# One layer of a hybrid trunk: squares and rotated inputs moved ahead, table copies spread and paired

## The chip, the cores and the metric

The kernel runs on one core of one Trainium2 chip. The metric is device time in microseconds (us) of one launch, which computes the whole layer. A core has five engines with a queue of instructions each: TensorE (PE; its weight loads are shown as PEld), VectorE (DVE), ScalarE (ACT), GpSimd (POOL) and SyncE (SP), which mostly issues DMA transfers. An engine takes its queue in order; engines wait for each other through semaphores. Matrix products land in PSUM, eight banks of 512 float32 per partition, and are evicted by DVE or ACT to SBUF, 128 partitions of on-chip memory.

## The reference

x is 2048 tokens (32 rows of a grid, 64 columns) by 1024, in float32; c is one vector.

```python
mod = silu(c) @ w_ada + b_ada
shift, scale, gate = split(mod, 3)
h = rmsnorm(x, norm_w) * (1 + scale) + shift
proj = h @ w_in + b_in      # na q,k,v,z (512 each); ml q,k,v,o,z (512 each); 16 gates
na = neighbourhood_attention(q, k, v, rpb) * silu(na_z)   # 8 heads of 64, window 8 x 16 on the grid
qk = silu(short_conv(concat(ml_q, ml_k)))                 # 5 taps along the tokens
hm = mlstm(forward) + flip(mlstm(flipped))                # 4 heads of 128, with sigmoid(ml_o)
ml = layernorm(hm) * ml_norm_w * silu(ml_z)
y = concat(na, ml) @ w_out
out = rmsnorm(x + gate * y) * final_norm_w
```

The attention adds a bias rpb[head, dy, dx] to the scores and masks what lies outside the window.

## The kernel before

Every large product is made in float32 precision of three products of half the width: a factor is split into a high part (hhi, whi) and the rest (hlo, wlo), and hi·hi, lo·hi and hi·lo are added up in PSUM. A k-step below is a slice of 128 of the inner 1024. The tokens are four groups (g = 0 to 3) of 512, or 16 tiles of 128.

**Token stage (`start`, 0 to about 145 us).** Group 0's rows are loaded, normalised and transposed on PE; the shift and scale columns are dot products on DVE (L264) and one-column products on PE (`mod`, L366); five `dense` products run ahead of them (L347). Its h is multiplied at once with two blocks of weights in PSUM (L418). Groups 1 to 3 go another way: a transposed copy of x (xt, `load_t`) is loaded, and h is made from it by `make_h` (L390): DVE multiplies with scale and with rb (L394), ACT adds the shift and rounds to hhi (L395), DVE takes the rest, hlo (L396). rb holds 1/rms of each token in every partition. It comes from four `square`s on ACT over plain rows of x (L260, one sum per token), `roots` (eleven small DVE operations, L270 and L1380 to L1395), four diagonal matrices on DVE (L285), and four products of ones with them on PE (L290). The diagonals and rb together are `spread`; rb is issued by its `run`.

A weight block is 256 columns; `vo_group(h, slot, g)` makes four tiles of 128 tokens by 256, 24 products each (L599 to L601, `tok_tile`), adds the bias on DVE (L671) and sends the stage tile stvo to DRAM (d_ck). After each eviction it takes a step of `self.chain`, which is how the next group's h (`next_h`) or weights (`next_w`) get between. `vo_first(g)` makes block 0's four tiles at once, k-step by k-step (L654), so that h may arrive block by block; `vo_group(0, 0, g, firsts)` then only evicts them. For group 0, `vo_group(2, 2, 0)` uses a third block, w_extra, split in two halves (L212 on ACT, L213).

**Token blocks (`tok_blocks`, to about 320 us).** Blocks 2 to 5 for all groups; the mLSTM's gates and decays run alongside as a chain (`decays`: dec loads from d_mneg on SP, mask on POOL, exponent on ACT). The attention's bias tables are made by DMA alone: d_e[head, column, dy, key column] gets rows of the bias at shifted places (`tables_columns`, 48 copies, L704), and d_t[head, query, key] gets rows of d_e (`tables_rows`, 72 copies, L726).

**Convolution blocks (`conv_blocks`, to about 480 us).** 32 tiles of 128 channels by 512 tokens (`pc`, 24 products); ACT moves each to u, DVE applies the taps (acc_k, acc_q, L982 to L984), ACT the silu (L986); k's are transposed on PE (kt, L995), moved by ACT (stk, L997) and stored by SP (L989, L999). `gated_out` loads rows of w_out (wraw, L910), multiplies them by gate on DVE and stores them (L918).

**mLSTM and the rest of the projections (to about 950 us)**, with products pq (L1042) between the small products of the chunks; `turn` transposes normalised chunks (ht, L1338) and `end` multiplies them into zt (L1344). **Attention and output (to the end):** units of two heads and 128 queries; scores pS (L1533), DVE adds the table and takes the minimum (L1541, pbuf; signs are turned), ACT exponentiates (L1542), PE transposes (pT) and multiplies with v (pO), then the output product y (L1621).

The order is partly a scheduler's (priorities follow the order in which the code calls), partly fixed: `manual_schedule` in the token stage keeps the order of the code, and `behind(step, other)` (L1161) puts a step behind another in order alone, without a semaphore.

## Time and profile before

| | us |
|---|---|
| three runs: median (lowest, highest) | 1324.9 (1324.34, 1331.62) |
| profiled execution | 1328.02 |
| its span, first to last instruction | 1326.2 |
| PE busy in it | 1282.2 |
| mean granted TensorE clock | 0.993 |

The three runs lie apart by more than the profiled one does from their median, so it is compared with itself first. In a row of the timeline the columns are the start, the duration, engine, line, operation, output and inputs, shape and count; in brackets the idle time of the engine just before and what ended it. A group's row gives the count with the shortest, median and longest duration in ns, and the first and last start. A row of windows gives, for a stretch, its length, each engine's busy time with its count, the granted clock of TensorE (1.00 is full), the DMA engines' busy share and GB/s. SPq and ACTq are queues that issue DMAs. x4 in a row joins four instructions that follow each other.

### The profile page before, as it was taken

The page shows a single profiled execution, that of the slowest core. Times are in us where ns is not written, and L with a number is a line of the kernel's source. Part 1 is how long each engine was busy: PE and PEld are TensorE (multiplying, and loading weights), DVE is VectorE, ACT ScalarE, POOL GpSimd, SP SyncE. Part 2 cuts the span into 40 slices and gives each one's busy share as a digit, 9 for nine tenths or more (in the row PEclk, how much of TensorE's full clock was granted, in tenths as well). Part 3 has the DMA queues.
Part 4 walks back from the last instruction along what each step waited for, and adds up shares of the span by engine and source line. Part 5 has one row for each costly group of instructions (what it writes and reads, how often), then busy time and mean ns, then how long its engine had stood idle before and what let it go on. Part 6 is the DMA issues. An engine that isn't in the chain of part 4 may idle for free.

```text
span 1326.2 us, 23060 instructions
## 1 busy us (share of the span) xinstructions
PE 1282.2 (97%) x8158; PEld 1099.5 (83%) x8158; DVE 791.9 (60%) x2445; ACT 536.6 (40%) x1175; POOL 194.9 (15%) x255
## 2 busy tenths in 40 slices
PE   8999999999999999999999999999998999999996
PEld 7998999998888787888888888888776777778785
DVE  6766352112556577166778778777547566766663
ACT  4543423553213322123323323333346555565561
POOL 0000102342000000111212002121202211212211
PEclk9999999999999999999999999999999999999998
DMA  9799966899276685445756767746779877868871
GB/s 365 256 293 319 239 199 144 219 246 231 77 174 183 167 215 158 147 132 165 211 151 212 229 181 215 234 140 194 196 236 240 214 184 195 201 175 194 191 185 48
DMA packets 236964, 263.86 MB, mean 199 GB/s; under 512 B 31142, under 2 KB 192294, under 8 KB 236850
## 3 DMA queue, kind: packets, MB, share of 16 engines
q1 hardware_dynamic: 152430, 189.92, 51.1%
q0 software_dynamic: 20496, 36.21, 11.1%
q10 hardware_dynamic: 63924, 36.27, 9.5%
q8 instruction: 64, 1.05, 0.3%
q14 instruction: 50, 0.41, 0.1%
HBM read 177.80 MB, written 92.72 MB: 204 GB/s over the span
## 4 chain that ended last, share of the span: by engine, by line
PE 62%; DMA 21%; issue 7%; DVE 5%; ACT 2%; POOL 1%; SPq 1%; ACTq 0%; POOLq 0%; DVEq 0%
PE pq L1042 19%; PE y L1621 10%; DMA tab<-d_t 5%; PE pc L600 4%; PE pc L599 4%; PE pc L601 4%; DMA d_ck<-dec 3%; PE pT L1561 2%; PE pO L1576 2%; DMA dec<-d_mneg 2%; PE pi L1283 2%; PE px L1281 2%; PE pS L1533 2%; PE pvo L599 2%; PE pvo L600 2%
## 5 line engine op out<-in xcount | busy, mean ns | idle before, releaser
L1042 PE MATMUL pq<-hhi,whi_a 128*128 128x512 f32 x512 | 208.7, 408 | 0.8 <-ACT u L947 0.8
L1042 PE MATMUL pq<-hlo,whi_a 128*128 128x512 f32 x512 | 209.0, 408 | 0.0
L1042 PE MATMUL pq<-hhi,wlo_a 128*128 128x512 f32 x512 | 207.4, 405 | 0.0
L1042 PEld LDWEIGHTS pq<-hhi,whi_a 128*128 128x128 f32 x512 | 97.3, 190 | 17.8 <-ACT u L947 1.3
L1042 PEld LDWEIGHTS pq<-hhi,wlo_a 128*128 128x128 f32 x512 | 97.1, 190 | 16.3
L1042 PEld LDWEIGHTS pq<-hlo,whi_a 128*128 128x128 f32 x512 | 97.1, 190 | 16.1 <-issue 0.5
L1563 ACT ACTIVATE pt<-pT 96x384 f32<-96x384 f32 (+3 forms) x128 | 65.8, 514 | 87.0 <-PE pT L1561 80.8
L1542 ACT ACTIVATE pbuf<-pbuf,mn 128x480 f32<-128x480 f32 (+5 forms) x128 | 76.0, 595 | 52.4 <-DVE mn L1541 52.2
L1621 PE MATMUL y<-hhi,whi_a 128*128 128x512 f32 x256 | 90.7, 416 | 0.5 <-ACT whi_a L1591 0.5
L1621 PE MATMUL y<-hhi,wlo_a 128*128 128x512 f32 (+1 forms) x272 | 90.6, 399 | 0.2 <-ACT y L1628 0.2
L1016 POOL TENSOR_TENSOR wlo_a<-rawq,whi_a 128x1024 fp32r<-128x1024 f32 x19 | 45.6, 2398 | 292.3 <-ACT whi_a L1015 265.1
L1541 DVE CUSTOM_DVE_ANT_0 pbuf<-pS,tab 128x480 f32<-128x480 f32 (+5 forms) x128 | 62.8, 540 | 37.3 <-PE pS L1533 30.9
L1286 ACT ACTIVATE num<-px,gtile 128x129 f32<-128x129 f32 x120 | 38.2, 365 | 113.5 <-PE px L1281 85.0
L1561 PEld LDWEIGHTS pT<-ident,pbuf 128*128 128x128 f32 (+2 forms) x416 | 50.8, 136 | 30.4 <-issue 9.4
L1561 PE MATMUL pT<-ident,pbuf 128*128 128x128 f32 (+2 forms) x416 | 67.1, 275 | 9.1 <-DVE pbuf L1553 6.6
L599 PE MATMUL pvo<-whi_b,hhi 128*128 128x256 f32 x224 | 63.9, 285 | 0.3 <-DVE gates L673 0.3
L1305 POOL TENSOR_TENSOR hm<-hm,ck 128x128 f32<-128x128 f32 x64 | 26.4, 412 | 254.9 <-DVE hm L1304 229.2
L889 ACT ACTIVATE dec<-dec,gtile 128x128 f32<-128x128 f32 x128 | 42.7, 393 | 50.7 <-POOL dec L882 46.6
L671 DVE TENSOR_TENSOR stvo<-pvo,brow 128x256 f32<-128x256 f32 x60 | 24.9, 421 | 64.1 <-PE pvo L601 47.0
L601 PE MATMUL pvo<-whi_b,hlo 128*128 128x256 f32 x224 | 63.1, 282 | 0.0
L600 PE MATMUL pvo<-wlo_b,hhi 128*128 128x256 f32 x224 | 63.1, 282 | 0.0
L634 DVE TENSOR_TENSOR stv<-pv,brow 128x256 f32<-128x256 f32 x32 | 13.0, 423 | 75.7 <-PE pv L601 35.4
(329 smaller groups left out, 3371.5 us busy)
## 6 DMA issues: line engine op xcount, KB each, us to landing
ck<-d_ck SPq DMA_DIRECT2D x64, 384.5 KB
rawq<-in_w_main_dram SPq DMA_DIRECT2D x28, 512.0 KB
raw<-in_w_main_dram SPq DMA_DIRECT2D x18, 512.0 KB
kv<-d_ck SPq DMA_DIRECT2D x64, 128.5 KB
dec<-d_mneg SPq DMA_DIRECT2D x32, 256.0 KB
d_ck<-dec ACTq DMA_DIRECT2D x32, 256.0 KB
d_qna<-qst ACTq DMA_DIRECT2D x32, 256.0 KB
xr<-in_x_dram POOLq DMA_DIRECT2D x15, 512.0 KB, 8.6
```

What stands on the lines that cost most here:

```text
L599: nc.tensor.matmul(ps, lhi(k), rhi(k), start=(k == 0), stop=False)
L600: nc.tensor.matmul(ps, lhi(k), rlo(k), start=False, stop=False)
L601: self.mark = nc.tensor.matmul(ps, llo(k), rhi(k), start=False, stop=(k == KT - 1))
L889: nc.scalar.activation(t[:, o, :], t[:, o, :], AF.Exp, bias=self.cols["g"][:, d, h, c : c + 1])
L1016: (eng or nc.gpsimd).tensor_tensor(lo[:, :, cs], raw, hi[:, :, cs].bitcast(F32), ALU.subtract)
L1042: self.mark = nc.tensor.matmul(patch_ps(ps) if patch else ps, w, self.htok(h, g, k, patch), start=(k == 0 and n == 0), stop=(k == KT - 1 a ...
L1286: nc.scalar.activation(num[:, d, :], px[:, d, :], AF.Copy, scale=self.cols["inter"][:, d, h, c : c + 1])
L1541: nc.vector.tensor_tensor_reduce(pt[:, :nk], ps, tabs[place[u]][j][:, :nk], 1.0, 3e38, ALU.add, ALU.min, mn)
L1542: nc.scalar.activation(pt[:, :nk], pt[:, :nk], AF.Exp, bias=mn, scale=-1.0, accum_out=sums[:, j : j + 1])
L1561: nc.tensor.transpose(ps[:cs, i, :], U[u][j][:, i * cs : (i + 1) * cs], self.ident)
L1563: nc.scalar.activation(t[:cs, :nch, :], ps[:cs, :nch, :], AF.Copy)
L1621: nc.tensor.matmul(y, m[:, k, :], w[k][:, cs], start=(k == 4 and n == 0), stop=(k == 3 and n == 2))
```

## The change

- Five more dense products at the start.
- Plain rows of group 1 are loaded by k-step 2 of group 0's products, into the space of group 2's hhi, and squared by ACT in k-steps 6 and 7; before, they were loaded at k-step 6 and squared after the last. Rows of groups 2 and 3, and the transposed x, get other places to lie in.
- h of a next group: blocks 0 and 1, 2 and 3, 4, 5 and 6 are made after the evictions of the four tiles of `vo_group(1, 1, g)`, block 7 at the start of `vo_first`; before, blocks 0 and 1, 2 and 3, 4 behind the third tile on, and 5 to 7 in `vo_first`. The next group's squares, roots, diagonals and rb are moved into `vo_first`.
- `next_w` splits the next weights on DVE instead of POOL.
- d_e and d_t hold the two heads of a unit side by side; a unit's table is one load of 128 x 2 nk instead of two. The copies that make them have other shapes and are issued four after each of the first thirty convolution tiles, behind the tile's last product; before, d_e's were issued in `tok_blocks`, d_t's of a kind in one go.
- q's scratch d_qna holds its four pieces of a query tile in one run of 2 KB.
- `turn` writes four transposes in the queries' order into one PSUM bank, and `end` takes the bank in one operation.

The places where the order moves. First PE in the first `vo_first` with k-steps of group 1 (pvo_4 to pvo_7 are its tiles, hhi and hlo its h). Before, around the second tile of `vo_group(1, 1, 1)`:

```order
L599 MATMUL pvo_5_1008<-whi_b,hhi_609 128x256
L600 MATMUL pvo_5_1008<-wlo_b,hhi_609 128x256
L601 MATMUL pvo_5_1008<-whi_b,hlo_610 128x256
L290 MATMUL rb_979<-diag_974,ones 128x128 x4
L599 MATMUL pvo_6_1039<-whi_b,hhi_609 128x256
```

and now, between k-steps 6 and 7 of `vo_first(1)`:

```order
L656 MATMUL pvo_6_825<-whi_a,hlo_621 128x272
L656 MATMUL pvo_7_826<-whi_a,hlo_621 128x272
L286 MATMUL rb_934<-diag_929,ones 128x128 x4
L656 MATMUL pvo_4_823<-whi_a,hhi_620 128x272
L656 MATMUL pvo_4_823<-wlo_a,hhi_620 128x272
```

rb of the next group stood behind the last k-step of `vo_first` and two tiles of 24 products; now it stands ahead of all of them. In `vo_group(2, 2, 0)` rb of group 1 moves from behind the second tile to behind the first.

Second DVE at the same place. Before, from the last block of h to the diagonals:

```order
L394 SCALAR_TENSOR_TENSOR h_7_861<-xt_611,gT,rb_667 128x512
L396 SCALAR_TENSOR_TENSOR hlo_610<-h_7_861,shT,hhi_609 128x512
L671 TENSOR_TENSOR stvo_1_950<-pvo_4_813,brow_129 128x2x128
L673 TENSOR_TENSOR gates<-pvo_4_813,bgate 128x16
L671 TENSOR_TENSOR stvo_1_950<-pvo_5_814,brow_129 128x2x128
```

and now:

```order
L390 SCALAR_TENSOR_TENSOR h_7_839<-xt_3_628,gT,rb_682 128x512
L392 SCALAR_TENSOR_TENSOR hlo_621<-h_7_839,shT,hhi_620 128x512
L266 TENSOR_SCALAR ssq_843<-ssq_843 128x4
L1378 TENSOR_SCALAR rst_916<-ssq_843 128x4
L1391 TENSOR_TENSOR nwt_x_919<-rst_916 128x4
```

The root and the diagonals of the next group (ssq, rst, diag) were behind the eight additions that evict `vo_first`'s tiles; they are now ahead of them.

Third SP in the convolution, around copies of d_e (one table) into d_t. Before:

```order
L208 DMA raw_1_4553<-in_w_main_dram 128x1024
L726 DMA d_t_77<-d_e_74 8x16x192 x8
L726 DMA d_t_80<-d_e_74 8x16x192 x8
L726 DMA d_t_83<-d_e_74 8x16x192 x8
L999 DMA d_ck<-stk_1_4612 128x4x128
L989 DMA d_ck<-acc_k_2_4543 128x4x128
```

and now:

```order
L1000 DMA d_ck<-stk_1_4350 128x4x128
L990 DMA d_ck<-acc_k_3_4355 128x4x128
L732 DMA d_t_75<-d_e_72 32x4x192 x4
L1000 DMA d_ck<-stk_2_4403 128x4x128
L732 DMA d_t_78<-d_e_72 32x4x192 x4
L1000 DMA d_ck<-stk_3_4454 128x4x128
```

24 copies in a row have become four between a tile's stores, over more tiles.

The diff, cut:

```diff
-        self.d_qna = d.tile([2, 2, 16, P, 2, P], F32, name="d_qna")
+        self.d_qna = d.tile([2, 16, P, 2, 2, P], F32, name="d_qna")
...
-        self.d_e = [d.tile([NH, 16, 15, nks[t]], F32, name=f"d_e{t}") for t in range(3)]
+        self.d_e = [d.tile([NH // 2, 16, 2, 15, nks[t]], F32, name=f"d_e{t}") for t in range(3)]
         nrs = [11, 15, 12]
-        self.d_t = [[d.tile([NH, P, nrs[r] * nks[t]], F32, name=f"d_t{r}{t}") for t in range(3)] for r in range(3)]
+        self.d_t = [[d.tile([NH // 2, P, 2, nrs[r] * nks[t]], F32, name=f"d_t{r}{t}") for t in range(3)] for r in range(3)]
...
-            held = self.hpools[3].tile([P, 4, D], F32, tag="hlo3", name="x_rows") if g == 3 else None
+            held = self.hpools[min(g + 1, 3)].tile([P, 4, D], F32, tag=(None, "hhi2", "hlo3", "hlo3")[g], name=f"xs_{g}") if g else None
             for j in range(4):
                 tt = 4 * g + j
-                xt[tt] = x_tile(f"x_{tt}") if held is None else held[:, j, :]
+                xt[tt] = held[:, j, :] if g else x_tile(f"x_{tt}")
...
-            held = self.hpools[g + 1].tile([P, 4, D], F32, tag=f"hhi{g + 1}", name=f"xt_{g}") if g < 3 else None
+            held = self.hpools[3].tile([P, 4, D], F32, tag="hhi3", name=f"xt_{g}") if g == 2 else None
             for j in range(4):
-                t = x_tile(f"xt_{g}_{j}") if held is None else held[:, j, :]
+                t = held[:, j, :] if g == 2 else x_tile(f"xt_{g}_{j}")
...
-        for _ in range(5):
+        for _ in range(10):
...
+        sums_1 = sums_x(range(4, 8))
...
+            if k == 2:
+                load_x(1)
             if k in (1, 5):
                 parts += self.raw_w(2, 2, (k // 4,))
-            if k == KT - 2:
-                load_x(1)
             if k >= KT - 2:
+                next(sums_1)
+                next(sums_1)
                 parts[k - KT + 2](nc.vector)
...
-        def next_h(tiles, run):
-            yield
+        def next_h(tiles):
+            for ks in ((0, 1), (2, 3), (4,), (5, 6)):
+                for low in [make_h(tiles, k) for k in ks]:
+                    low()
+                yield
+
+        def first_next_h(tiles, run):
             run()
             yield
-            for k in (0, 2):
+            for k in (0, 2, 4):
                 for low in (make_h(tiles, k), make_h(tiles, k + 1)):
                     low()
                 yield
+            make_h(tiles, 6)()
 
         def next_w():
             for part in self.raw_w(2, 0):
                 yield
-                part()
+                part(nc.vector)
...
                 for k, _ in enumerate(self.vo_first(g)):
-                    if k < 3:
-                        make_h(now, k + 5)()
+                    if k == 0:
+                        make_h(now, 7)()
+                    if k < 4:
+                        next(sums, None)
                     if k == 2:
                         self.flush()
                         next(fills, None)
-                    if k >= 4:
-                        next(sums, None)
+                    if k == 3 and g == 1:
+                        load_x(3)
+                        load_t(3)
+                    if k == 4 and tiles:
+                        self.token_tiles(g + 1)
+                        spreads[g + 1], run = spread(tiles, roots(tiles, ssqs[g + 1]))
+                    if k == 6 and tiles:
+                        run()
+                self.vo_group(0, 0, g, self.firsts)
                 if tiles:
-                    self.token_tiles(g + 1)
-                if g == 1:
-                    load_x(3)
-                    load_t(3)
-                self.vo_group(0, 0, g, self.firsts)
+                    self.chain = next_h(tiles)
+                else:
+                    self.load_bias(2)
+                    self.chain = next_w()
+                self.vo_group(1, 1, g)
             else:
                 self.vo_group(0, 0, 0, firsts)
                 self.vo_group(1, 1, 0, seconds)
-            if tiles:
-                spreads[g + 1], run = spread(tiles, roots(tiles, ssqs[g + 1]))
-                self.chain = next_h(tiles, run)
-            else:
-                self.load_bias(2)
-                self.chain = next_w()
-            if g:
-                self.vo_group(1, 1, g)
-            else:
+                load_x(2)
+                load_t(2)
+                spreads[1], run = spread(tiles, roots(tiles, ssqs[1]))
+                self.chain = first_next_h(tiles, run)
                 tops = [self.tq.tile([P, GT], F32, tag="tp", name=f"pvo_2_{o}") for o in range(2)]
                 self.vo_group(2, 2, 0, brow=brow, tops=tops)
                 self.wslot.pop()
-                load_x(2)
-                load_t(2)
             for _ in self.chain:
                 pass
-            if tiles:
-                make_h(tiles, 4)()
...
-            (nc.sync if h == 2 else nc.scalar).dma_start(dst, st[:, :, 0:257])
+            (nc.scalar if h == 0 else nc.sync).dma_start(dst, st[:, :, 0:257])
...
-    def tables_columns(self, ct):
-        nc = self.nc
-        c0 = (0, 16, 48)[ct]
-        k0 = (0, 8, 40)[ct]
-        for i in range(16):
-            c = c0 + i
-            start = min(max(c - 8, 0), GRID_W - 16)
-            dx = start - c + 15
-            nc.sync.dma_start(self.d_e[ct][:, i, :, start - k0 : start - k0 + 16], self.d_rneg[:, :, dx : dx + 16])
+    def tables_columns(self):
+        nc = self.nc
+        for ct in range(3):
+            c0 = (0, 16, 48)[ct]
+            k0 = (0, 8, 40)[ct]
+            for i in range(16):
+                c = c0 + i
+                start = min(max(c - 8, 0), GRID_W - 16)
+                dx = start - c + 15
+                dst = self.d_e[ct][:, i, :, :, start - k0 : start - k0 + 16].rearrange("h e a k -> (e a) h k")
+                src = self.d_rneg.rearrange("(h e) a k -> (e a) h k", e=2)[:, :, dx : dx + 16]
+                yield self.behind(nc.sync.dma_start(dst, src), self.mark)
...
+        for ct, rt, r in itertools.product(range(3), range(3), range(8)):
...
+            dst = self.d_t[rt][ct][:, r * 16 : (r + 1) * 16, :, j0 : j0 + 8 * nk].rearrange("h q e n -> (q e) h n")
+            src = self.d_e[ct][:, :, :, dy : dy + 8, :].rearrange("h c e a k -> (c e) h (a k)")
+            yield self.behind(nc.sync.dma_start(dst, src), self.mark)
...
+        copies = itertools.chain(self.tables_columns(), self.tables_rows())
...
+                    for _ in range(4):
+                        next(copies, None)
...
-            if o % 2 == 0:
-                self.ht = self.ms.tile([P, 2, CH], F32, tag="ht", bufs=1, name=f"ht_{h}_{c}")
-            ps = self.ht[:, o % 2, :]
-            nc.tensor.transpose(ps, hm[gi][:, o, :], self.perm)
-            self.ends.append(lambda: end(c, ps))
-
-        def end(c, ps):
-            gi, o = divmod(c, 4)
-            ts = slice(o * 32, (o + 1) * 32)
-            nc.vector.scalar_tensor_tensor(zt[gi][:, :, ts], ps.rearrange("p (a q) -> p a q", a=4), self.mlw[:, h : h + 1], zt[gi][:, :, ts], ALU.mult, ALU.mult)
+            if o == 0:
+                self.ht = self.ms.tile([P, GT], F32, tag="ht", bufs=1, name=f"ht_{h}_{gi}")
+            nc.tensor.transpose(patch_ps(self.ht)[:, 2 * o : 2 * o + 2], hm[gi][:, o, :], grid_rows(self.ident))
             if o == 3:
-                src = zt[gi]
-                out = self.d_mix[4 * gi : 4 * gi + 4, :, h].rearrange("a p q -> p a q")
-                self.stores.append(lambda: nc.scalar.dma_start(out, src))
+                ps = self.ht
+                self.ends.append(lambda: end(gi, ps))
+
+        def end(gi, ps):
+            z = zt[gi].rearrange("p a q -> p (a q)")
+            nc.vector.scalar_tensor_tensor(z, ps, self.mlw[:, h : h + 1], z, ALU.mult, ALU.mult)
+            src = zt[gi]
+            out = self.d_mix[4 * gi : 4 * gi + 4, :, h].rearrange("a p q -> p a q")
+            self.stores.append(lambda: nc.scalar.dma_start(out, src))
...
-        def load_tab(u, j):
+        def load_tab(u):
             b, ct = units[u]
             nk = geo[b][4]
-            (nc.gpsimd if u < 2 else nc.sync).dma_start(tabs[place[u]][j][:, :nk], self.d_t[PR_T[b // 4]][PC_T[b % 4]][2 * ct + j])
+            src = self.d_t[PR_T[b // 4]][PC_T[b % 4]][ct].rearrange("q e k -> q (e k)")
+            (nc.gpsimd if u < 2 else nc.sync).dma_start(tabs[place[u]][:, : 2 * nk], src)
...
-                    if u in follows:
-                        load_tab(follows[u], j)
+                if u in follows:
+                    load_tab(follows[u])
```

## The prediction

> **What bounds the kernel now.** I read the page first, then TensorE's waits, then windows, then the order of single engines where a wait lies. The page:

> ```profile
> span 1326.2 us, 23060 instructions
> PE 1282.2 (97%) x8158; PEld 1099.5 (83%) x8158; DVE 791.9 (60%) x2445; ACT 536.6 (40%) x1175; POOL 194.9 (15%) x255
> ```

> TensorE (PE) is busy for 97%. No product is removed in number that matters, so all there is to win is its idle time, 1326.2 − 1282.2 = 44 us, and stretches at a lower clock. This execution took 1328.0 us, 1.8 more than its span and 3.1 above the median of the three runs, 1324.9; I sum against it and carry the difference over to the median. What ends PE's idle time, in the places that the change touches (waited for: us in all, times, longest):

> ```profile
> PE mod L366 <- DMA mod_hi<-in_w_mod_dram: 3.7, 1, 3.7
> PE pv L599 <- DVE stv L634: 2.7, 1, 2.7
> PE kt L995 <- ACT acc_k L986: 2.7, 2, 2.5
> PE pvo L654 <- ACT hhi L395: 1.5, 4, 0.4
> PE pvo L600 <- POOL wlo_a L213: 1.1, 1, 1.1
> PE ht L1338 <- DVE zt L1344: 0.9, 1, 0.9
> ```

> The idle time is spread over many short waits, each with its own cause. Windows show what a wait costs beyond itself:

> ```profile
> core 0: us, PE busy (x) PEld busy (x) DVE busy (x) ACT busy (x) POOL busy (x), PEclk, DMA share, GB/s
> 45.30:48.71 3.41, 1.69 (x12) 1.27 (x11) 2.72 (x5) 3.13 (x4) 0.00 (x0) 1.00 1.00 383
> 48.73:52.14 3.41, 3.41 (x18) 3.41 (x18) 2.91 (x11) 3.32 (x7) 0.00 (x0) 0.50 1.01 396
> 448.00:451.50 3.50, 3.50 (x10) 2.75 (x9) 1.91 (x5) 1.78 (x3) 0.00 (x0) 0.51 0.92 281
> ```

> After 3.41 us in which PE was busy for only 1.69, the next 3.41 us had a granted clock of 0.50, so 1.7 us of work was lost. The same follows the kt wait (448.0 to 451.5).

> **The warm-up.** Ten dense products instead of five; each is two records:

> ```profile
> 1.56 4.37 PE L347 MATMUL dense<-big,ident 128*128 128x240 f32 x10 [1.56 <-POOL stvo L660]
> 9.59 1.20 PE L366 MATMUL mod<-cact,mod_hi 128*128 128x1 f32 x5 [3.65 <-DMA mod_hi<-in_w_mod_dram]
> 21.31 0.67 PE L366 MATMUL mod<-cact,mod_hi 128*128 128x1 f32 x5
> ```

> Twenty records at 0.44 us end at 10.3 us at the low clock and before 9.59 if the clock rises half-way, so at worst they delay the mod products by 0.7 us. Five mod products take 1.20 us early and 0.67 us once the clock is up. About thirty of them run early, which gives at most 3 us. But the stretch to 42 us also waits for weights to arrive, so I take −1.3 (0 to −3).

> **Tail of group 0.** Four squares of group 1's rows go in front of the last weight splits on ScalarE.

> ```profile
> 45.58 0.78 ACT L387 ACTIVATE hhi<-tp,shT,gT 128x512 fp32r<-128x512 f32 x1 [1.88 <-DVE shT L264]
> 46.92 1.05 ACT L212 ACTIVATE w_extra<-raw 128x1024 fp32r<-128x1024 f32 x1
> 47.87 1.05 ACT L260 ACTIVATE junk<-x 128x1024 bf16<-128x1024 f32 x1
> 48.81 0.20 ACT L260 ACTIVATION_READ_ACCUMULATOR junk<-x 128x1 f32 x1
> 48.00 1.22 DVE L213 TENSOR_TENSOR w_extra<-raw,w_extra 128x1024 fp32r<-128x1024 f32 x1 [0.25 <-ACT w_extra L212]
> 52.98 0.16 DVE L270 TENSOR_SCALAR ssq<-ssq 128x4 f32<-128x4 f32 x1
> 55.23 0.87 DVE L285 TENSOR_SCALAR diag<-ident,rst 128x128 f32<-128x128 f32 x4
> ```

> A square with its read takes 1.14 us (47.87 to 49.01). Two of them, 2.3 us, go into the 1.88 us that ScalarE idles before 45.58, so h's last block is 0.4 us later: +0.4. The other two push the second w_extra split from 46.92 to about 49.7 and DVE's subtraction from 48.00 to 50.8. All ten additions of PSUM tiles stand behind it on DVE, and then the root (eleven small operations, 2.25 us from 52.98 to 55.23) and the four diagonals. So the diagonals end near 58.6 instead of 56.1.

> **The token stage, groups 1 to 3.** Here the transposing product rb (diagonals times ones), on which every h of the next group waits, moves forward on PE: for group 1 from behind the second tile to behind the first, for groups 2 and 3 from behind the second tile of vo_group(1,1,g) to ahead of the last k-step of vo_first. PE takes its queue in order, so it now stands at rb until the diagonals are there, with the last products queued behind. Three places:

> - rb of group 1: the first w_extra tile starts 0.4 us later than 52.08 (where the first window below begins) and has 24 products of 0.121 us (14.92 / 123), so PE is at rb at 55.4; diagonals at 58.6: a wait of 3.2 us.
> - rb of group 2: h's block 7 is made at the head of vo_first. DVE needs 0.74 + 0.75 us per block (below), eight blocks and the additions between them from 59, then ScalarE does hhi and four squares (4.6), DVE the root (2.2) and diagonals (0.9). That ends near 83. PE starts vo_first at 67.6 (58.6 plus rb plus three tiles of 2.9) and does seven k-steps of 12 products by 78: a wait of 5.0 us.
> - rb of group 3: the same chain, but DVE is ahead by the wait before: 2.4 us by the same addition.

> ```profile
> L396 DVE SCALAR_TENSOR_TENSOR hlo<-h,shT,hhi 128x512 fp32r<-128x512 f32 x24 | 17.5, 751 | 10.3 <-ACT hhi L395 9.5
> L394 DVE SCALAR_TENSOR_TENSOR h<-xt,gT,rb 128x512 f32<-128x512 f32 x24 | 17.3, 741 | 0.0
> 52.08:67.00 14.92, 14.84 (x123) 1.00 0.64 216
> 67.00:93.00 26.00, 25.03 (x200) 1.00 0.98 272
> 93.00:119.00 26.00, 24.49 (x193) 1.00 1.11 332
> 119.00:143.80 24.80, 23.59 (x186) 1.00 1.06 297
> ```

> Against these 10.6 us stand the short waits of PE for h (blocks 5 to 7 were made during vo_first), which go, since blocks 0 to 6 now lie a tile ahead. (The last four rows are windows of PE alone: busy us and, in brackets, products.) At 0.121 us per product, the 200, 193 and 186 products of the other three would take 24.3, 23.4 and 22.6 us: 6.6 us of waits. Net +4.0. From both sides: if the squares end early enough for no wait at rb, −6.6; with all 10.6 and half of the old waits left, +7.3. I take +4.0 because each link has a row.

> The wait for group 2 covers a whole 3.41 us stretch; by the window at 45.3 the clock halves after it, +1.7. The first wait, 3.2 us, would do so by that row as well (0 to +3.4 for both; I take one). [...]

> **Weights of the next block to DVE.**

> ```profile
> 142.80 4.72 POOL L213 TENSOR_TENSOR wlo_a<-raw,whi_a 128x1024 fp32r<-128x1024 f32 x2 [8.01 <-ACT whi_a L212]
> 147.57 0.39 PE L600 MATMUL pvo<-wlo_a,hhi 128*128 128x256 f32 x1 [0.67 <-POOL stvo L660]
> ```

> On DVE one takes 1.22 us (row at 48.00) against 2.36, in idle gaps between additions. PE's two waits go, 1.1 for wlo_a (its row above) and 0.67: −1.8 (0 to −1.8).

> **Token blocks.** The 48 copies d_e<-d_rneg and the first d_t copies leave SP's queue here.

> ```profile
> 312.67 1.42 DVE L634 TENSOR_TENSOR stv<-pv,brow 128x256 f32<-128x256 f32 x4 [12.01 <-DMA d_vna<-stv]
> L704 SPq DMA_DIRECT2D d_e<-d_rneg x48: 608/613/1470, 165.4 to 236.2; - x48
> ```

> The 2.7 us wait of pv is a store issued late on SP, behind the decays' loads. Nine copies of d_t, each as long as those of d_e (0.6 us or more), stood between those loads; without them the chain is a few us earlier: −2.0 (0 to −2.7).

> **Convolution.** SP's two bursts of 24 copies become four copies after each of thirty tiles, d_e's included.

> ```profile
> 445.56 19.73 SPq L726 DMA_DIRECT2D d_t<-d_e  x24
> 436.28 0.36 SPq L999 DMA_DIRECT2D d_ck<-stk  x1
> ...
> 437.77 0.53 SPq L918 DMA_DIRECT2D d_wo<-wraw  x1
> 438.84 0.40 PE L601 MATMUL pc<-hhi,wlo_a 128*128 128x512 f32 x1
> 439.07 0.40 PE L599 MATMUL pc<-hhi,whi_a 128*128 128x512 f32 x1
> ```

> A burst shuts SP for 19.7 us, 0.82 us per copy, and what is queued behind it, loads and the stores that free buffers, comes late; around them lie kt's waits, 2.7 us, and the half clock, 1.7 us. Spread, SP is shut for 4 × 0.82 = 3.3 us at a time; a tile of 24 products at 0.23 us lasts 5.6. I take −3.7 of the 4.4. In the sixteen tiles of k the stores of stk and acc_k and a load and a store of wraw come to it, 2.0 us from 436.28 to 438.30: 5.3 of 5.6, little room. Above, rival C is the bound.

> **mLSTM.** Four evictions of 128x128 become one of 128x512, by the nearest row (L394) 741 ns.

> ```profile
> L1344 DVE SCALAR_TENSOR_TENSOR zt<-ht,mlw,zt x60: 331/344/352, 612.3 to 936.0; 128x128 f32<-128x128 f32 x60
> ```

> DVE gains 16 × 0.64 us, which hides in its idle time (40% of the span). PE waited 0.9 us for zt: −0.5 (+0.5 to −0.9, as the one bank must be emptied before the next group's first transpose).

> **Attention tables.** Two loads of a unit become one, issued after the second reduction instead of one after each.

> ```profile
> DMA tab<-d_t: 5.1, 8
> ```

> DVE waited 5.1 us for tables. Half the issues free SP; the first half of a pair is asked for one reduction (0.5 us) later. I take −1.5 (+1.0 to −3.0). d_qna's longer runs touch no wait of these rows: 0.

> **Sum.** −1.3 + 0.4 + 4.0 + 1.7 − 1.8 − 2.0 − 3.7 − 0.5 − 1.5 = −4.7 us. From 1328.0 that is 1323.3 for this execution; from the median, 1320.2: **1320 us**.

> **Rivals.**
> A, no wait at rb. If DVE and ScalarE run ahead of PE through vo_first, rb costs nothing and the 6.6 us of waits are won: the sum is 0.4 − 1.3 − 6.6 − 1.8 − 2.0 − 3.7 − 0.5 − 1.5 = −17.0, 1308 us. For it: blocks 0 to 6 do lie earlier. Against it: the chain of squares, root and diagonals is 4.6 + 2.25 + 0.87 = 7.7 us from block 7's hhi, whatever its start.
> B, the waits only change place. The long chains behind pv and kt are of latency, not of issues; if both waits come back elsewhere and the clock loss too, 5.7 us are lost from the sum: 1325–1326 us, no change.
> C, slower: SP becomes the bound in the convolution. The copies' new shapes (30x4x16 and 32x4xN instead of 8x15x16 and 8x16xN) have no row. Above (5.6 − 2.0) / 4 = 0.90 us per copy SP falls behind on each of k's sixteen tiles, and PE with it. At 1.0 us that is 0.4 × 16 = 6.4 us, and the −3.7 is lost: 1330 us; at 1.15 us, 1340. For it: single copies went up to 1.47 us (L704's row).

> **Chances.** Forecast 0.50 (1313 to 1326), A 0.22, B 0.14, C 0.14. A measurement tells 0.5%, 6.6 us, from no change, so faster is below 1318.3. Of the forecast's half about 0.18 lies below it: faster 0.18 + 0.22 = 0.40, same 0.32 + 0.14 = 0.46, slower 0.14. Range: from A's 1308 to the beginning of C, 1307 to 1330.

> **What would show it.** Waits of PE at the rb line of about 3, 5 and 2 us for DVE's diag, with a granted clock near 0.5 after the second; no wait of pvo for hhi or hlo in vo_first; no PE wait for POOL's wlo_a; no burst above 4 us on SP and no wait of kt between 340 and 480 us; spacing of SP's copies there near 0.8 us. If rb's line shows no wait, A was right; if pc or kt wait in every tile, C.

## The result, and the profile after

| | us |
|---|---|
| the change: median of 9 runs (lowest, highest) | 1319.24 (1316.99, 1323.55) |
| the kernel before: median of 9 runs | 1331.21 (1324.19, 1334.17) |
| ratio, 95% interval | 0.9924 (0.9898 to 0.9949) |
| profiled execution of the change, its span | 1317.95, 1316.2 |

By the ratio the change is faster by 0.8%, about 10 us (the medians lie 12 us apart); 1320 was forecast. The nine runs of before contain the three of the first table and six more, most of them longer. On another chip, one of those where the experiments ran, the unaltered change took 1322.34 and the kernel before 1345.21: 0.9825 (0.9793 to 0.9857). So the change's own time is steady within some 10 us over the chips, and before's is not (1324 to 1352); the section on the experiments comes back to this, but no profile of before was taken where it took 1345.

The page of the change, and the longest of TensorE's (PE's) waits in it (waited for: us in all, times, longest):

```profile
span 1316.2 us, 22879 instructions
PE 1279.0 (97%) x8168; PEld 1100.9 (84%) x8168; DVE 791.4 (60%) x2398; ACT 534.5 (41%) x1175; POOL 188.8 (14%) x251
...
PE rb L286 <- DVE diag L281: 6.8, 3, 3.5
PE pT L1560 <- DVE pbuf L1552: 4.5, 4, 1.9
PE pvo L414 <- ACT hhi L383: 2.6, 1, 2.6
```

The waits of pv for stv, of kt for acc_k, of pvo for wlo_a and of ht for zt, which stood in the list of before, are gone. New at the top is rb, three times, as the prediction said (6.8 us against 10.6), and a wait of 2.6 us for hhi in group 0, which it did not see.

The stages, counted from PE's first product (1.56 us into the span) and cut at the starts of products in the traces: the first product with w_extra (the end of group 0's own part), the last product of the last `vo_first`, the first and last pv, the first pc, the first pq, the first y, the last y. The rows below the first three are the experiments'.

| us | to w_extra | token stage | to pv | pv | pc to pq | pq to y | y to end |
|---|---|---|---|---|---|---|---|
| before | 50.5 | 80.2 | 98.4 | 93.8 | 191.1 | 485.3 | 314.6 |
| before, again | 49.3 | 80.1 | 99.0 | 99.9 | 188.8 | 484.6 | 318.9 |
| the change | 50.1 | 86.3 | 95.9 | 90.9 | 186.4 | 482.1 | 312.5 |
| the change, again | 50.2 | 83.8 | 95.9 | 90.9 | 187.6 | 484.5 | 316.9 |
| squares after | 48.3 | 87.6 | 95.9 | 90.9 | 190.1 | 483.4 | 313.7 |
| rb after a tile | 49.7 | 87.0 | 95.9 | 90.9 | 190.2 | 484.0 | 316.8 |
| five dense | 50.4 | 86.3 | 95.9 | 90.9 | 187.8 | 485.2 | 312.9 |
| bursts | 49.8 | 83.7 | 95.9 | 90.9 | 209.4 | 496.1 | 315.4 |
| squares ahead | 50.3 | 78.0 | 96.7 | 90.9 | 190.1 | 484.0 | 312.1 |
| roots first | 49.6 | 79.6 | 96.1 | 90.9 | 187.4 | 483.4 | 315.0 |
| old token stage | 49.8 | 82.7 | 100.8 | 90.9 | 190.5 | 482.7 | 313.5 |
| split on GpSimd | 50.5 | 86.3 | 96.9 | 90.9 | 186.4 | 484.6 | 315.6 |
| columns back | 50.3 | 83.4 | 95.9 | 92.0 | 186.5 | 480.9 | 314.6 |

In the first pair of profiles the change loses 6.1 us in the token stage and wins 15.4 us in the stages behind it. The column pv is the firmest: 90.9 us, without a wait, in all ten profiles in the table whose kernel has d_e's copies in the convolution, against 93.8 and 99.9 before. The last three columns vary by 4 us and more between kernels whose code there is the same; a difference of 2 us in them in one pair of profiles says nothing. So the 5.3 us that the first pair shows in the last two columns, half of its gain, lie within this scatter, and no experiment here traces them to an edit.

Where the token stage loses. Windows of PE alone (length, busy us with the products' count, granted clock, DMA share, GB/s) of the change:

```profile
47.30:50.70 3.40, 3.34 (x15) 0.50 0.88 326
53.00:57.60 4.60, 2.70 (x23) 1.00 0.96 291
57.60:61.00 3.40, 3.40 (x18) 0.50 1.01 232
78.00:81.50 3.50, 1.03 (x9) 1.00 0.77 123
81.50:88.30 6.80, 5.76 (x26) 0.50 0.98 369
```

Four 3.4 us windows at half clock (57.6, 81.5 and the one behind it, and 47.3) behind the waits at rb and hhi. At the granted 0.50 each costs up to 1.7 us beside the wait itself, an estimate from half of PE's 3.40 us. The one at 47.3 is no loss against before, which has its own at 48.73 (shown in the prediction).

### The profile page after: what moved, and what is told of

Read it like the earlier page. It is cut to its first block, busy times and chain, and to the rows that moved or that the text cites. A ratio compares the mean times of both kernels' runs of the same rounds, so it can differ in the third digit from the quotient of the medians.

```text
span 1316.2 us, 22879 instructions
## 1 busy us (share of the span) xinstructions
PE 1279.0 (97%) x8168; PEld 1100.9 (84%) x8168; DVE 791.4 (60%) x2398; ACT 534.5 (41%) x1175; POOL 188.8 (14%) x251
## 3 DMA queue, kind: packets, MB, share of 16 engines
q1 hardware_dynamic: 142670, 190.45, 50.8%
q8 instruction: 65, 1.06, 0.3%
## 4 chain that ended last, share of the span: by engine, by line
PE 74%; issue 7%; DMA 5%; DVE 4%; POOL 1%; ACT 1%; POOLq 0%; SPq 0%; DVEq 0%; ACTq 0%
PE pq L1043 18%; PE y L1620 12%; PE pc L602 4%; PE pc L603 4%; PE pc L601 4%; PE pO L1575 3%; PE pT L1560 3%; PE pvo L601 2%; PE pv L603 2%; PE pvo L603 2%; PE pvo L602 2%; PE pS L1532 2%; PE pv L602 2%; PE pv L601 2%; PE pi L1282 2%
## 5 line engine op out<-in xcount | busy, mean ns | idle before, releaser
L1043 PEld LDWEIGHTS pq<-hhi,whi_a 128*128 128x128 f32 x512 | 96.8, 189 | 17.4 <-ACT u L948 1.3
L1043 PEld LDWEIGHTS pq<-hhi,wlo_a 128*128 128x128 f32 x512 | 96.7, 189 | 17.4 <-POOL wlo_a L1017 0.8
L1043 PEld LDWEIGHTS pq<-hlo,whi_a 128*128 128x128 f32 x512 | 96.8, 189 | 16.1 <-issue 0.5
L1541 ACT ACTIVATE pbuf<-pbuf,mn 128x480 f32<-128x480 f32 (+5 forms) x128 | 75.9, 594 | 50.5 <-DVE mn L1540 50.5
L1560 PEld LDWEIGHTS pT<-ident,pbuf 128*128 128x128 f32 (+2 forms) x416 | 50.7, 136 | 27.5 <-ACT pt L1562 7.1
L601 PE MATMUL pvo<-whi_b,hhi 128*128 128x256 f32 x224 | 63.9, 285 | 0.0
L890 ACT ACTIVATE dec<-dec,gtile 128x128 f32<-128x128 f32 x128 | 41.3, 391 | 49.8 <-POOL dec L883 41.8
L673 DVE TENSOR_TENSOR stvo<-pvo,brow 128x256 f32<-128x256 f32 x60 | 25.0, 422 | 59.7 <-PE pvo L603 42.6
```

The lines of the kernel that those rows point to most:

```text
L601: nc.tensor.matmul(ps, lhi(k), rhi(k), start=(k == 0), stop=False)
L890: nc.scalar.activation(t[:, o, :], t[:, o, :], AF.Exp, bias=self.cols["g"][:, d, h, c : c + 1])
L1043: self.mark = nc.tensor.matmul(patch_ps(ps) if patch else ps, w, self.htok(h, g, k, patch), start=(k == 0 and n == 0), stop=(k == KT - 1 a ...
L1541: nc.scalar.activation(pt[:, :nk], pt[:, :nk], AF.Exp, bias=mn, scale=-1.0, accum_out=sums[:, j : j + 1])
L1560: nc.tensor.transpose(ps[:cs, i, :], U[u][j][:, i * cs : (i + 1) * cs], self.ident)
```

## Experiments

Each kernel is the change with one edit. The landmarks are those of the table.

### Group 1's squares behind the last products

```diff
             if k >= KT - 2:
-                next(sums_1)
-                next(sums_1)
                 parts[k - KT + 2](nc.vector)
...
         load_t(1)
+        for _ in sums_1:
+            pass
```

> The change with one part undone: the four squares of group 1's rows run on ScalarE after group 0's last products, as before the change, instead of in k-steps 6 and 7 (the rows are still loaded ahead). Theory (the squares, queued in front of hhi's last block, wait for their rows and hold hhi up): PE's wait for hhi near 43 us falls from 2.65 to 1.0 or less, the half-clock stretch at 47.3 to 50.7 goes, the first product with w_extra starts at about 48.5 instead of 51.6; rb of group 1 then waits 1 to 2 us longer; the token stage (end of the last vo_first, 137.9) ends 2 to 3 us earlier. Rival (the early load of the rows takes DMA time from what hhi needs): the wait stays at 2 us or more and w_extra starts at 51 or later.

Measured: 1322.46 (1319.05 to 1323.76). The wait for hhi fell to 0.8 us and w_extra came 1.8 us earlier, at 49.9 and not at 48.5. The half clock did not go: it lay from 46.7 to 50.1 in this run. The stage ended at 137.5, only 0.4 earlier: the waits at rb rose from 6.8 to 8.2 us. In the change, ScalarE's rows show why hhi was late:

```profile
41.81 1.06 ACT L256 ACTIVATE junk<-xs 128x1024 bf16<-128x1024 f32 x1 [1.69 <-DMA xs<-in_x_dram]
42.78 0.19 ACT L256 ACTIVATION_READ_ACCUMULATOR junk<-xs 128x1 f32 x1
43.15 1.06 ACT L256 ACTIVATE junk<-xs 128x1024 bf16<-128x1024 f32 x1 [0.19 <-DMA xs<-in_x_dram]
44.11 0.19 ACT L256 ACTIVATION_READ_ACCUMULATOR junk<-xs 128x1 f32 x1
44.21 1.04 ACT L208 ACTIVATE w_extra<-raw 128x1024 fp32r<-128x1024 f32 x1
45.15 0.76 ACT L383 ACTIVATE hhi<-tp,shT,gT 128x512 fp32r<-128x512 f32 x1
```

The two squares did not fill an idle gap. They stood in it waiting for their rows, and hhi behind them. The theory holds for the wait, but not for the half clock; and what PE gains there it waits for at the diagonals.

### rb behind a tile for groups 2 and 3

```diff
-        def next_h(tiles):
+        def next_h(tiles, run):
+            run()
+            yield
             for ks in ((0, 1), (2, 3), (4,), (5, 6)):
...
-                    if k == 6 and tiles:
-                        run()
```

> The change with one part moved: rb of groups 2 and 3 stands behind the first tile of the next weight block instead of ahead of vo_first's last k-step; h of the next group starts one tile later. Theory (PE stands at rb for the diagonals, and the clock falls after it): the waits of 3.5 and about 1.4 us at groups 2 and 3's rb and the two half-clock stretches from 81.5 to 88.3 go; PE waits again for h's blocks 5 to 7 in vo_first, at most 1.5 us a group; the token stage ends 4 to 6 us earlier (137.9 to about 133), the whole 4 to 6 us shorter than the change. Rival (h on DVE is the bound, wherever rb stands): vo_first waits for h by as much as rb did, and the stage ends within 1.5 us of 137.9.

Measured: 1325.52 (1321.11 to 1332.32), the stage's end at 138.3 against 137.9. The theory fell. PE no longer waits at rb of groups 2 and 3, but for the evictions instead:

```profile
PE pvo L601 <- DVE gates L675: 6.3, 2, 3.2
PE rb L286 <- DVE diag L281: 1.9, 1, 1.9
PE pvo L656 <- DVE stvo L673: 1.3, 3, 0.5
```

DVE's rows in the same run:

```profile
79.58 0.17 DVE L266 TENSOR_SCALAR ssq<-ssq 128x4 f32<-128x4 f32 x1 [3.83 <-ACT junk L256]
...
82.55 0.42 DVE L673 TENSOR_TENSOR stvo<-pvo,brow 128x256 f32<-128x256 f32 x1
82.88 0.17 DVE L675 TENSOR_TENSOR gates<-pvo,bgate 128x16 f32<-128x16 f32 x1
```

On DVE the root stands ahead of the additions that empty `vo_first`'s PSUM tiles, and waits 3.83 us for the squares. Whether PE waits at rb or for those banks, the same chain ends the wait: hhi's last block, four squares, root, diagonals. Of the rival, too, only half is right: not h itself, but the squares among it are what is late.

### Squares of groups 2 and 3 one block further ahead

```diff
                 for low in [make_h(tiles, k) for k in ks]:
                     low()
+                next(sums, None)
                 yield
...
-                    if k < 4:
-                        next(sums, None)
```

> The change with the squares of groups 2 and 3 one block further ahead: one behind each of the four steps that make h of the group before, where ScalarE idles 1.8 us between pairs, instead of all four in vo_first. Theory (the wait at rb of groups 2 and 3 is the chain hhi's block 7, four squares, root, diagonals; the squares, 4.7 us, are the piece that can leave it): ssq's start on DVE comes right after hlo's block 7, at about 76.2 instead of 80.0; rb of group 2 waits under 0.5 us instead of 3.5, rb of group 3 not at all, no half clock at 81.5 to 88.3; the last vo_first ends 6 to 8 us earlier, at 130 to 132. Rival (h on DVE is the bound, wherever the rest stands): the end stays within 1.5 us of 138 as it did when rb was moved; or the squares' rows land late and hhi waits behind them on ScalarE.

> The change itself, unaltered, as the yardstick on the chip of the next three runs. Both theories: the same landmarks to 1 us (w_extra's first product at about 51.5, end of the last vo_first at about 138), and a ratio to the kernel before of 0.985 to 0.995.

Measured on one chip: 1317.36 (1315.82 to 1318.61) against 1322.34 (1320.06 to 1326.3) for the unaltered change; the ratio to before is 0.9784 (0.9758 to 0.9811). The token stage takes 78.0 us instead of 83.8. (The repeat of the change itself missed its expectation twice: its last `vo_first` ended at 135.6 and not at 138, and its ratio was 0.9825.) ScalarE's rows:

```profile
65.22 1.38 ACT L391 ACTIVATE hhi<-h,shT 128x512 fp32r<-128x512 f32 x2 [0.77 <-DVE h L390]
66.51 1.04 ACT L256 ACTIVATE junk<-xs 128x1024 bf16<-128x1024 f32 x1
67.46 0.19 ACT L256 ACTIVATION_READ_ACCUMULATOR junk<-xs 128x1 f32 x1
68.43 1.38 ACT L391 ACTIVATE hhi<-h,shT 128x512 fp32r<-128x512 f32 x2 [0.78 <-DVE h L390]
```

and what is left of PE's waits from 50 to 140 us:

```profile
PE pvo L659 <- DVE stvo L676: 2.0, 3, 1.4
PE rb L286 <- DVE diag L281: 1.9, 1, 1.9
```

A square fits between two pairs of hhi, which keep waiting for DVE as before (0.77 us, it was 1.8). The root of group 2 starts at 74.9 (80.0 in the first profile of the change), rb of groups 2 and 3 waits no more, and no window there is at half clock. The theory holds. This kernel beats both.

### Group 1's root ahead of the evictions, on top of that

```diff
+                spreads[1], run = spread(tiles, roots(tiles, ssqs[1]))
                 self.vo_group(0, 0, 0, firsts)
                 self.vo_group(1, 1, 0, seconds)
                 load_x(2)
                 load_t(2)
-                spreads[1], run = spread(tiles, roots(tiles, ssqs[1]))
```

> As the run with the squares further ahead, and group 1's root and diagonals ahead of the additions that evict group 0's tiles on DVE. Theory: the diagonals of group 1 are ready at about 54.1 instead of 57.0, PE's first wait at rb (1.9 us) goes to under 0.3, and the stage ends 2 us earlier than that run's. Rival: the evictions, 3 us later, hold PE up over PSUM, or the stage tile's store; no gain or a loss up to 1 us.

Measured: 1315.8 (1315.28 to 1318.16), which can't be told from the run before it. PE's wait of 1.9 us at rb stays, with another name:

```profile
PE pvo L659 <- DVE stvo L676: 2.1, 3, 1.5
PE rb L286 <- DVE stvo L676: 1.9, 1, 1.9
```

Now the evictions are late and the diagonals are not. The rival was right: what delays rb is the sum of both on DVE.

### The token stage as before, the rest of the change

Edit: the loads of rows, squares, `next_h`, the order of root, rb and `vo_group` and the queue of one store as they were before; `next_w` still splits on DVE.

> The token stage (rows, squares, rb, order of h) as before the change; all the rest of the change kept: ten dense products, weights split on DVE, paired tables and their spread copies, one-bank transposes. Theory (the new token stage costs 5.6 us at its end, 137.9 against 132.3 in the profiles): the last vo_first ends at 132 to 133, and the whole is 4 to 6 us faster than the change. Rival (the later stages take the lead back, as their waits on DMA come due earlier): the whole is within 1.5 us of the change.

Measured: 1324.83 (1321.12 to 1325.22), against 1322.34 (1320.06 to 1326.3) for the change on the same chip, so the two can't be told apart. The theory fell, though its landmark was near: the last `vo_first` ended 1.6 us earlier than the change's. From there to the first pv it took 100.8 us instead of 95.9. PE's waits in it from 132 to 236 us:

```profile
PE ps_ends L802 <- DVE ends L799: 2.0, 2, 1.1
PE pvo L596 <- DVE wlo_a L209: 0.8, 1, 0.8
```

From 160 to 170 us the mean granted clock is 0.83 (1.00 from 150 to 160 and from 170 to 180), 1.7 us of the ten. With them these waits are most of the 4.9 us. The 2.0 us at ps_ends do not come from the split on DVE. DVE stands 6.60 us for a load of the gate's weights (ga), ahead of the operations that make ends, and three of the four loads of ga are issued 18 us after the first. Rows of this run, then of the change:

```profile
135.37 0.43 SPq L553 DMA_DIRECT2D ga<-in_w_gt_dram  x1
153.63 2.02 SPq L553 DMA_DIRECT2D ga<-in_w_gt_dram  x3
160.55 0.49 DVE L562 TENSOR_SCALAR gsum<-ga,cact 128x512 f32<-128x512 f32 x1 [6.60 <-DMA ga<-in_w_gt_dram]
```

```profile
134.97 1.87 SPq L559 DMA_DIRECT2D ga<-in_w_gt_dram  x4
155.90 0.87 DVE L568 TENSOR_SCALAR gsum<-ga,cact 128x512 f32<-128x512 f32 x2
```

The change issues all four at once, and DVE does not wait for them; in the first profile of before it waits 4.54 us. So the order of the token stage also sets when these loads go out, a part of the change that the prediction did not see; how it does so was not followed. At any rate the token stage's loss and the next stage's gain belong together: the two stages taken as one are 3.7 us shorter with the new order (83.8 + 95.9 against 82.7 + 100.8, before rounding).

### Five dense products

```diff
-        for _ in range(10):
+        for _ in range(5):
```

> The change with five dense products instead of ten. Theory (the stretch from 15 to 43 us is bound by the shift and scale columns and their loads, not by PE): the first product of group 0 starts at about 18.4 instead of 15.1, but the first product with w_extra within 1 us of 51.6. Rival (PE's early clock counts to the end): w_extra starts 2.5 us or more later.

Measured: 1323.17 in one run. The first product of group 0 starts at 18.4 against 15.1 and w_extra's at 51.9 against 51.6: 3.0 of the 3.3 us are gone by then. The theory holds; the five products are worth 0.3 us or nothing.

### The weights' split back on GpSimd

```diff
-                part(nc.vector)
+                part()
```

> The change with the next weights' split back on GpSimd. Theory: PE waits 1.5 to 2.5 us for wlo_a right after the last vo_first, and the first pv product comes that much later against the end of the last vo_first (95.9 us between them in the change, 98.4 before). Rival (the additions on DVE hide it either way): within 0.5 us of 95.9.

Measured: 1325.08 in one run. From the last `vo_first` to pv it takes 96.9 us against 95.9: 1.0 us, half of what was expected, and neither theory's number. PE waits 0.6 us for POOL there.

### Table copies in bursts

```diff
-                    for _ in range(4):
+                    for _ in range(24 if (8 * i + 4 * sub + g) % 6 == 5 else 0):
                         next(copies, None)
```

> The change with the 120 table copies issued 24 in a row after every sixth convolution tile instead of four after each tile; shapes and their sum are the same. Theory (a shut SP delays the loads and stores of the convolution): SP's rows show bursts of 15 to 20 us, kt's or pc's waits come back with 2 to 5 us, and the stretch from the first pc to the first pq takes 188.5 to 191 us instead of 186.4. Rival (the gain came from what left the stage or from the shapes): the stretch stays within 1 us of 186.4.

Measured: 1354.99 in one run. The convolution takes 209.4 us and the stage behind it up to the first ht 110.0 instead of 96.8. Rows of SP (SPq, issues) and PE's waits in this run, then SP in the change:

```profile
355.80 20.93 SPq L709 DMA_DIRECT2D d_e<-d_rneg  x24
...
PE kt L996 <- ACT acc_k L987: 16.5, 4, 9.2
PE pq L1043 <- ACT whi_a L1016: 10.0, 1, 10.0
```

```profile
L709 SPq DMA_DIRECT2D d_e<-d_rneg x48: 779/792/919, 327.9 to 402.2; - x48
L732 SPq DMA_DIRECT2D d_t<-d_e x72: 528/599/1346, 406.3 to 498.4; - x72
427.66 2.53 SPq L732 DMA_DIRECT2D d_t<-d_e  x4
```

The theory's mechanism is right and its price was far too low. Four bursts shut SP for 17 to 21 us each; stores that free stk and acc_k and the weights for pq come late, and PE waits 27 us in all; around these waits the clock stands at half in three stretches, of 6.8, 10.2 and 13.7 us, and the mean granted clock of the execution is 0.980 (0.990 in the change's). Spread, four copies take 3.3 us (d_e) or 2.5 us (d_t).

### d_e's copies back in the token blocks

```diff
                     parts[g - 1](self.nc.vector)
+            if n > 0:
+                for _ in self.tables_columns(n - 1):
+                    pass
```

> The change with the 48 copies from d_rneg to d_e back in the token blocks, ahead of the decays' loads on SP; the 72 others stay spread over the convolution, now its first 18 tiles. Theory (pv's wait of 2.7 us came from a store of d_vna that stood on SP behind decays' loads that the copies had made late): from first to last pv product 92.5 to 94 us instead of 90.85, with PE waiting for stv again. Rival (the d_t copies between the decays' loads, not the d_e ones ahead of them, did it): it stays at 90.85 to 91.3.

Measured: 1317.57 in one run. pv takes 92.0 us, with a wait of 0.5 us for stv, between the two theories. So copies ahead of the decays' loads bring back some of the wait, not all. That the rest comes from the d_t copies among those loads is not shown: they were not tried alone. The convolution, without d_e's copies, takes 186.5 us.

### The kernel before, once more

> The kernel before, unaltered, profiled once more, since its time lay between 1324 and 1352 us on the chips so far while the change lay between 1317 and 1326. Theory (SP's bursts of 24 table copies make it sensitive: each shuts SP for 20 us while the convolution's stores and loads wait): what it has over the first profile of before lies between the first pc and the first ht, as waits of kt and half-clock stretches (187 us from pc to pq in the change; 191 in the first profile; 195 to 215 here). Rival (a slower chip or memory): the surplus is spread over all stages.

Measured: 1334.81. The theory fell. The convolution, with its bursts, took 188.8 us, less than in the first profile. The surplus is in pv and from y to the end (table). PE's wait there and its cause on DVE:

```profile
PE pv L599 <- DVE stv L634: 6.9, 1, 6.9
...
316.08 1.42 DVE L634 TENSOR_TENSOR stv<-pv,brow 128x256 f32<-128x256 f32 x4 [16.21 <-DMA d_vna<-stv]
```

It is the same wait as the 2.7 us of the first profile, 4.2 us longer, and two half-clock windows follow (mean granted clock of the execution 0.989, of the first profile 0.993). By these rows one thing that varies in before between the two profiles is when the decays' loads and the store of d_vna behind them on SP get through. The change has taken that wait away, which may be part of why its gain is larger on the other chips. The 4.3 us from y to the end were not followed.

### Two loads per table

```diff
-        def load_tab(u):
+        def load_tab(u, j):
...
-            (nc.gpsimd if u < 2 else nc.sync).dma_start(tabs[place[u]][:, : 2 * nk], src)
+            (nc.gpsimd if u < 2 else nc.sync).dma_start(tabs[place[u]][:, j * nk : (j + 1) * nk], src)
```

> The change with two loads per table in the attention, each issued after its own reduction, out of the paired scratch; 54 issues more. Theory (one load instead of two relieves SP and the DMA queues): from the first y product to the end it takes 1 to 2.5 us longer than the change, DVE waits 1.5 to 4 us more for tables. Rival (the table loads were never late enough to matter; the change's gain there came from elsewhere or was chance): within 1 us, and as the first half is asked for earlier, perhaps less.

Measured: 1372.63 (1365.72 to 1379.08). This kernel doesn't compute the same: where the next unit's rows are longer, its first half is written over the second half of the present one before that is read, so scores get other biases, and DVE waits 42.6 us for tables in the middle of units. It says nothing about the question, which stays open. What the other runs tell of it is in the next section.

## Why the prediction was right, step by step

The time and the cause of the waits at rb were right, and in the first pair of profiles the sign of each stage. The sum was too small: −4.7 us, where the first pair of profiles has −10.1 and the medians −12.0. That 1320 was met is also luck with the runs it was counted from: 1324.9 was the low end of what before takes, and that made up for the missing half of the sum. Faster by over 0.5% had 0.40, no change 0.46; by the ratio, 0.76% (0.51% to 1.02%), the first came true, though 1319.24 is not below the 1318.3 that the prediction drew from 1324.9.

- **Warm-up, −1.3.** 0.3 or nothing by the run with five. The doubt in that step, that the stretch waits for other things, was the whole of it.
- **Tail of group 0, +0.4.** Failed. "Two of them, 2.3 us, go into the 1.88 us that ScalarE idles" took the rows as there; the squares had to wait for them and started at 41.8 and 43.2, and PE waited 2.65 us for hhi instead of 0.4 more than before (0.8). In the repeat of the change that wait was 1.0 us, so it seems to hang on when the DMA delivers. It cost 0.4 us at the end of the stage by the run with the squares after, since rb waited anyway.
- **Waits at rb, 3.2, 5.0 and 2.4.** 1.90, 3.51 and 1.4 us. The mechanism was right, the sizes were too high by a third: group 1's diagonals were ready at 57.0 and not at 58.6, and PE came to group 2's rb at 79.0 and not at 78, held up by the half clock from 57.6 on.
- **Half clock, +1.7.** Mis-sized: three windows behind the two waits in the first profile, 4.6 us (half of PE's busy time in them, 3.40 and 5.76), one in the repeat, 1.7. Net, the stage lost 6.1 and 3.6 us against +5.7 forecast (4.0 and 1.7). That the first profile meets the 5.7 is luck in part: the waits at rb were 3.8 us too high and the clock 2.9 too low. What is left for the old waits that went is 6.8 + 4.6 − 6.1 = 5.3 us, in the repeat 4.9, by this estimate, against the 6.6 taken.
- **Split on DVE, −1.8.** 1.0 us by the run that undoes it. The stage behind the last `vo_first` is 2.5 us shorter than in the first profile of before; there the new order adds its own part through the gate's loads, which the prediction did not have.
- **Token blocks, −2.0.** −3.0 against the first profile of before, −9.1 against the second.
- **Convolution, −3.7.** −4.6 in the first pair. Over all profiles the change's stage takes 186.4 to 190.5, before's 188.8 and 191.1; on the average some 1.5 us are left of it. "Little room" was right: in four of the runs a kt wait of 1.9 to 2.4 us and a half-clock window near 390 to 400 us come back (0.50 from 398.2 to 401.6 with the squares after), at a time when d_e's copies, the stores of k and the gate's loads share SP.
- **mLSTM, −0.5.** The wait of ht for zt is gone; the new eviction takes 745 ns (741 was taken). The stage's scatter hides more than that.
- **Tables, −1.5.** Not shown, perhaps wrong in sign. The loads land later (rows of before, then of the change, then the wait in its repeat):

```profile
DMA tab<-d_t: 5.1, 8
DMA to landing us min/median/max: 4.7/5.1/6.6
```

```profile
DMA tab<-d_t: 3.6, 4
DMA to landing us min/median/max: 2.7/7.1/9.5
```

```profile
DMA tab<-d_t: 19.0, 11
```

  In the eleven profiles of kernels with paired tables in one load DVE waits 3.6 to 19.0 us for them, 13 on the average; in the two of before 5.1 and 7.3. The step counted the issues saved and the later request, and not that one load for both heads lands 2 us later than a load for one (medians of 7.1 and 5.1 us in the rows above). From y to the end the time is 312 to 317 us against 314.6 and 318.9: no loss shows either. The new layout of d_qna, taken as 0, was not tried alone.
- **Rival A** (no wait at rb) did not come true, but the run with the squares ahead reaches its condition for groups 2 and 3, and some 5 of its 12 us. **B** (waits change place) was true within the token stage, as the run with rb moved shows, not for pv, and for kt in the four runs where its wait came back. **C** (SP the bound) fell: copies took 0.79 and 0.60 us, below the 0.90 at which it would begin.

## What to carry to other kernels

When a wait is found at one instruction, write down the whole chain that ends it, across engines, and shorten the chain: moving the waiting product changed the wait's name, moving four squares into another engine's idle time removed it. Look at how many small transfers stand together on a queue, and not only at their sum: the same 120 copies on SP gave a convolution of 209.4 us with 24 in a row, and of 186.4 and 187.6 us with four at a time. Judge a stage by several profiles before crediting an edit with 2 us: identical code differed by 4.

## What the runs showed of the hardware beyond what was expected

```profile
54.15:57.57 3.42, 1.52 (x14) 1.00 1.03 314
57.57:60.99 3.42, 3.42 (x19) 0.50 1.03 234
```

```profile
52.06:55.48 3.42, 2.84 (x24) 1.00 0.70 222
55.48:58.89 3.41, 2.09 (x18) 1.00 1.12 253
58.89:62.31 3.42, 3.42 (x30) 1.00 0.98 278
```

In the first profile one window holds the whole wait, with PE busy for 1.52 of 3.42 us, and the next is at half clock. In the repeat the wait lies in two windows, with PE busy for 2.84 and 2.09 us, and no half clock follows. After the second wait there was one window at half clock (82.80 to 86.20 us) instead of two, and the token stage took 83.8 us instead of 86.3. That the place of a wait in the windows decided its price is an inference from these two profiles.

The traces of the first pair of profiles were cut in this way from 30 us to the end, each on its own grid, into 379 windows for before and 376 for the change. Until the products end, six windows at full clock are followed by half clock: PE was busy for 50%, 40% and 39% of them in before (at 45.32, 444.68 and 963.50 us) and for 15%, 44% and 29% in the change (at 43.92, 54.16 and 78.05 us). In every other window at full clock up to there PE was busy for 54% or more. Of the seven windows at half clock, six had PE busy for 99% or more and were followed by full clock; the one at 81.47 us had 69% and was followed by another at half. PE's busy time is the profile's, with modelled ends.
